# A pool of its own for the whole gates' tiles in a gated hybrid attention block

## The chip, the cores and the metric

The kernel runs on one core of one Trainium2 chip. The metric is the device time of one execution in microseconds (us). The engines are TensorE (PE in the profile, PEld its weight loads), VectorE (DVE), ScalarE (ACT), GpSimd (POOL) and SyncE (SP, which here issues the DMAs). SBUF is the on-chip memory of 128 partitions; PSUM holds the matmuls' results in 8 banks of 128 x 512 fp32.

## The reference

One transformer block in fp32 on 1024 tokens of width 1024. Three attention branches of width 512 run on the normed input: A, a differential attention of 4 heads; B, a dilated window attention with three groups of 4 heads, whose outputs are mixed by the softmax of their log-sum-exps; and C, an attention to 256 memory slots. Each branch has a projection to the full width and a sigmoid gate for every channel; the gated sum goes through an output matrix, and a SwiGLU feed-forward part follows.

```python
wts = jax.nn.softmax(jnp.stack(lses, axis=2), axis=2)                       # the merge of B
out_b = jnp.sum(wts[..., None].astype(bv.dtype) * jnp.stack(outs, axis=2), axis=2)
...
branches = jnp.einsum('btgc,gcd->btgd', jnp.stack([out_a, out_b, out_c], axis=2), w_branch[l])
gates = jax.nn.sigmoid(h @ w_gate[l] + b_gate[l]).reshape(b, t, N_BRANCHES, d)
x = x + jnp.sum(gates * branches, axis=2) @ w_out[l]
h2 = rms_norm(x, norm_ffn[l])
x = x + (jax.nn.silu(h2 @ w_ffn_gate[l]) * (h2 @ w_ffn_up[l])) @ w_ffn_down[l]
```

## The kernel before, in words

Activations are kept transposed: 8 tiles of 128 channels by 1024 tokens, in two halves c of 512. An fp32 operand is split into a rounded high part and a low remainder (`split`, L257: ACT casts the high part at L259, another engine subtracts at L260; for weights L156 and L157), and a product takes three matmuls for each pair of operands (L191 to L193). A pair of high and low is a tile of 4 KB a partition, called `t4`, and the pools `big` (16 tiles) and `a4` (20 tiles) hold such tiles.

The work goes through the input projections, the gates' products (their sums before the sigmoid are stored in DRAM, `gates[n]`, 24 arrays of 512 KB), the attentions C, A and B, the branch projections, the output matrix and the feed-forward part. Products of branches A and C run among the heads of B as fillers.

At the end of each of B's four heads comes the merge (L975 to L1003). Its small weights go to DRAM and come back spread over all partitions as one tile `W` of 128 x 3072 (L998, 1.5 MB). DVE multiplies three head tiles `u` by it (L1000), adds them in two steps (L1002), and the sum is spilled to DRAM (L1003). After the fourth head the pools of the attention are closed (`att.close()`, L1006), and the pools `pb` (6 PSUM banks), `ev` and `a4` are allocated in the memory that they leave.

Then `gated_first(d)` (L1094) runs for d = 0 to 7. It loads two whole gates into tiles of `a4` (`whole_gate`, L1088: the DMA at L1090, the sigmoid on ACT at L1091), multiplies the mix, which holds branch A, by the first (L1097), evicts two banks of branch C's product from PSUM times the second (L1099), and adds that to the mix (L1100). With 2 banks of another pool there are 8, so the products of four values of d fit before an eviction must free one; a block d takes 24 matmuls. After it comes branch B for c = 0: its input `oT[1, k, c]` is loaded from the spill (L1147, tile `c`) and split on ACT and POOL; its gates are loaded for each half (L1072), and evicted at L1085 and added at L1086. The output weights `wo[d]` (L1112) and the feed-forward's operands `h2` follow in `big` and `a4`. In the last stage (`down`, seven products over 11 pairs of k of the matrix w_fd) the right operands take tiles of `a4` as well, beside 8 tiles of w_fd itself, loaded at L1227.

The order of instructions on each engine is set when the program is built: a scheduler simulates the work and orders each engine's instructions by it, taking a wait for memory into account where a new tile covers the bytes of an old one. On the chip each engine goes through its list in order. All DMAs of this part are issued by SP in one queue, and their completions are told by 8 semaphores in turn.

In the built program of before, W of the last merge takes bytes 146,624 to 158,912 of each partition and `a4` begins at 146,944. The tiles of the first and the seventh d's first loads lie at 146,944 and 151,040, inside W's bytes.

Of the kernel before, what the change touches and what calls it, by code (L numbers as in the profile page):

```python
# [30 lines left out]
LAMBDA_INIT = 0.8 - 0.6  # L31
BIG = 1e30

A4 = 20
EV_BUFS = {"g": 5, "s": 4, "c": 2, "ws": 2}

EARLY = 3
# [40 lines left out]
def hybrid_block_kernel(ctx: ExitStack, tc: tile.TileContext, xT, memT, w_ab, w_cq, w_kv,  # L78
# [3 lines left out]
    def pool(name, bufs=1, space=None, stack=ctx):  # L82
        kw = {} if space is None else {"space": space}
        if space is not DRAM:
            kw["reuse_waits"] = "tile"
        return stack.enter_context(tc.tile_pool(name=name, bufs=bufs, **kw))
# [14 lines left out]
    V, G = nc.vector, nc.gpsimd  # L101
# [25 lines left out]
    gx, gf = (const.tile([P, KT], F32, name=f"g{m}") for m in "xf")  # L127
# [37 lines left out]
    big = pool("big", 16)  # L165
# [91 lines left out]
    def split(dst, src, eng):  # L257

        nc.scalar.copy(dst[:, 0], src)  # L259
        eng.tensor_sub(dst[:, 1], src, dst[:, 0].bitcast(F32))  # L260
# [57 lines left out]
    with ExitStack() as pst:  # L318
# [196 lines left out]
        for u in (U_AV, *range(U_AQK, U_AQK + 4, 2), *range(U_BV, U_BV + 6, 2), *range(U_BQK, U_BQK + 12, 2)):  # L515
# [9 lines left out]
            if u in (U_BV, U_BV + 2, U_BV + 4):  # L525
                x = ("T1", "T3", "T4")[(u - U_BV) // 2]
# [54 lines left out]
    def early_sum():  # L581
        return wp.tile([P, 512], F32, name="eg", bufs=3)
# [204 lines left out]
    with ExitStack() as st:  # L787
# [8 lines left out]
        mix, oT = [], {}  # L796
# [57 lines left out]
        for h in range(BH):  # L854
            st_mc = bp.tile([P, 3, 2, 8], F32, name="mc", bufs=2)
            U = []
            for g in range(3):
# [58 lines left out]
                elif g == 1:  # L916
                    for q4 in range(2):
                        op = ps_tile(opp, "op")
                        for r2 in range(2):
                            r = 2 * q4 + r2  # L920
# [87 lines left out]

    pb = pool("pb", 6, PSUM)
    ev = pool("ev")  # L1010
    a4 = pool("a4", A4)
    turn = [0]

# [4 lines left out]
    def t4(pl, dt=F32R):  # L1018
        return pl.tile([P, 2, 512], dt, name="t4")

    def t2(name):
        return ev.tile([P, 512], F32, name=name, bufs=EV_BUFS[name])
# [5 lines left out]
    def right(pl, src, eng):  # L1028
        t = t4(pl)
        split(t, src, eng)  # L1030
        return t

    def rights(blocks, pls, gain, scale):

        rs, t2s = {}, []
        n = len(blocks)

        def make(name, srcs):  # L1040
            rs[name] = [right(pls[name][i], x, V) for i, x in enumerate(srcs)]

        for i, ((b11, b12), (b21, b22)) in enumerate(blocks):
            for b, g in ((b12, i), (b22, i + n)):
                V.scalar_tensor_tensor(out=b, in0=b, scalar=gain[:, g:g + 1], in1=scale, op0=ALU.mult, op1=ALU.mult)
            V.tensor_sub(b11, b12, b11)
            t2s.append(t2("s"))
            V.tensor_sub(t2s[-1], b22, b11)
            rs.setdefault("T2", []).append(right(pls["T2"][i], t2s[-1], V))
        for (b11, b12), (b21, b22) in blocks:  # L1050
            V.tensor_sub(b12, b22, b12)
        make("T3", [b[0][1] for b in blocks])
        for i, ((b11, b12), (b21, b22)) in enumerate(blocks):
            V.tensor_sub(b21, t2s[i], b21)
        make("T4", [b[1][0] for b in blocks])
        make("T1", [b[0][0] for b in blocks])
        make("22", [b[1][1] for b in blocks])
        return rs
# [7 lines left out]
    def blocks_of(ts_):  # L1066
        return [[[t[:, c] for c in range(2)] for t in p_] for p_ in ts_]
# [8 lines left out]
    x1 = mix  # L1076
# [26 lines left out]
    mh, wo, pss = {}, {}, {}  # L1103
# [4 lines left out]
    def load_out(d):  # L1108

        raw = wp.tile([P, 1024], F32, name="raw", bufs=3)  # L1110
        nc.sync.dma_start(out=raw.rearrange("p (k m) -> p k m", m=P), in_=w_out[d])
        wo[d] = [right(a4, raw[:, i * 512:(i + 1) * 512], G) for i in range(2)]  # L1112

    def out_block(d, c):

# [16 lines left out]
    def row_scale(c):  # L1132
        return rsqrt(ev, pss[c][0], D, [P, 512], ("g", "g"), EV_BUFS["g"])

    h2 = {"11": [], "21": []}

    def norm_first(k, r, rst):
        i = k + 4 * (r == "21")
        V.scalar_tensor_tensor(out=x1[i][:, 0], in0=x1[i][:, 0], scalar=gf[:, i:i + 1], in1=rst, op0=ALU.mult, op1=ALU.mult)
        h2[r].append(right(big if k % 2 else a4, x1[i][:, 0], V))  # L1140

    for d in range(KT):
        gated_first(d, load_pieces(w_br[2 * KT + d], 4, P))
    for c in range(2):
        for k in range(4):
            o = t2("c")
            nc.sync.dma_start(out=o, in_=spill[1][:, k, CS[c]])  # L1147
            oT[1, k, c] = right(a4, o, G)
    for d in range(KT):
        gated(1, d, 0, load_pieces(w_br[KT + d], 4, P))  # L1150
        split_mix(d, 0, big)
    for d in range(KT):
        load_out(d)
        out_block(d, 0)
        gated(1, d, 1, load_pieces(w_br[KT + d], 4, P))
# [3 lines left out]
    rst = row_scale(0)  # L1159
    for n, d in enumerate(reversed(range(KT))):  # L1160
        out_block(d, 1)
        norm_first(n % 4, ("11", "21")[n // 4], rst)
# [50 lines left out]
    rst = row_scale(1)  # L1213
# [1 line left out]
        low[0] = V if f else G  # L1215
        ahead(f)
    bl = blocks_of([(x1[k], x1[k + 4]) for k in range(4)])
    h2 |= rights(bl, {**{x: [a4] * 4 for x in ("T2", "T1", "T3", "T4")}, "22": [big] * 4}, gf, rst)


    wd, groups = {}, [range(k, min(k + 2, HF)) for k in range(0, HF, 2)]
# [73 lines left out]
    for d, ps in enumerate(down("T1", s1_of)):  # L1295
        V.tensor_add(u3s[d], ps, u3s[d])
        store_out(1, d, 1, u3s[d], G)
        x = early_sum()
# [91 lines left out]
```

## Time and profile before

| what | value |
|---|---|
| three runs | 2110.09, 2111.51, 2114.27 us |
| median | 2111.51 us |
| the profiled execution | 2107.51 us, of it 2105.7 us span |
| granted TensorE clock, mean | 0.985 |
| busy, share of the span | PE 95%, PEld 82%, DVE 65%, ACT 44%, POOL 53% |
| DMA traffic | 300.37 MB, mean 143 GB/s |

How to read it: times of single instructions come from the profiled execution, which is one run of its own; the median is over three other runs. Busy shares are means over the whole span, in which the stages differ. The clock is told as a share of 2.4 GHz, and 0.5 is 1.2 GHz. A row of the chain of waits names what the end of the program was waiting for at that moment, in order of time.

### The profile page before, as it was taken

How to read it: one execution, taken by the hardware profiler on the slowest of the kernel's cores; microseconds unless marked ns; L12 is line 12 of the kernel's file. 1: busy time of each engine (PE TensorE's matmuls, PEld its weight loads, DVE VectorE, ACT ScalarE, POOL GpSimd, SP SyncE). 2: the span in 40 equal slices, each digit the busy share in tenths (PEclk: the TensorE clock that was granted, in tenths of full speed). 3: DMA queues.
4: the chain of work that ended last, by engine and by line, in shares of the span. 5: the costliest groups of instructions: out<-in, count | busy, mean ns of one | idle time of the engine just before them, and what ended most of it. 6: DMA issues, size and time to landing. Idle time of an engine off the chain costs nothing.

```text
span 2105.7 us, 31371 instructions
## 1 busy us (share of the span) xinstructions
PE 1990.1 (95%) x11384; PEld 1716.8 (82%) x11384; DVE 1363.7 (65%) x2148; ACT 917.0 (44%) x1839; POOL 1114.4 (53%) x766
## 2 busy tenths in 40 slices
PE   6799999999999889899989997999999999999999
PEld 5799999999977677678768785777788888888887
DVE  8975543566575799997354436633977667579961
ACT  5434322344344566664535655532523323344441
POOL 5685644666753576665445223820165554545764
PEclk9899999999999999999999998999999999999999
DMA  6263343323143333254866537642344323255441
GB/s 228 82 214 111 106 141 115 101 91 131 71 161 128 122 113 97 80 162 152 265 228 221 174 112 281 198 144 80 136 146 149 106 85 125 96 174 216 145 152 69
DMA packets 134730, 300.37 MB, mean 143 GB/s; under 512 B 19120, under 2 KB 43184, under 8 KB 134064
## 3 DMA queue, kind: packets, MB, share of 16 engines
q1 hardware_dynamic: 134576, 298.37, 42.0%
q8 instruction: 90, 1.47, 0.3%
q14 instruction: 64, 0.52, 0.1%
HBM read 204.58 MB, written 89.54 MB: 140 GB/s over the span
## 4 chain that ended last, share of the span: by engine, by line
PE 40%; DVE 4%; DMA 3%; issue 1%; ACT 1%; POOL 1%; SPq 0%; DVEq 0%; ACTq 0%; POOLq 0%
PE pb L191 9%; PE pb L193 9%; PE pb L192 9%; PE mm L191 4%; PE mm L192 4%; PE mm L193 4%; DMA W<-wd 1%; DVE u L1000 1%; PE mm L1130 1%; PE op L939 1%; DVE t L1086 0%; PE tp L293 0%; DVE t L260 0%; DVE u L1002 0%; PE op L910 0%
## 5 line engine op out<-in xcount | busy, mean ns | idle before, releaser
L211 POOL TENSOR_TENSOR wl<-raw,wh 128x512 fp32r<-128x512 f32 x204 | 282.0, 1394 | 186.4 <-ACT wh L210 163.4
L191 PE MATMUL pb<-t,wh 128*128 128x512 f32 x795 | 308.4, 391 | 15.2 <-DVE t L1099 15.2
L192 PE MATMUL pb<-t,wh 128*128 128x512 f32 x795 | 310.9, 392 | 1.9 <-DVE t L260 1.9
L193 PE MATMUL pb<-t,wl 128*128 128x512 f32 x795 | 311.0, 391 | 0.0
L191 PE MATMUL mm<-t,wh 128*128 128x512 f32 x657 | 265.0, 404 | 7.9 <-ACT wh L210 5.4
L193 PE MATMUL mm<-t,wl 128*128 128x512 f32 x657 | 260.1, 397 | 1.2 <-POOL wl L211 1.2
L192 PE MATMUL mm<-t,wh 128*128 128x512 f32 x657 | 260.8, 397 | 0.0
L210 ACT CAST wh<-raw 128x512 fp32r<-128x512 f32 x216 | 129.9, 618 | 205.3 <-PE pb L192 95.8
L191 PEld LDWEIGHTS pb<-t,wh 128*128 128x128 f32 x795 | 150.1, 189 | 47.3 <-DVE t L1099 15.7
L480 PE MATMUL sp<-wh,t 128*128 128x256 f32 x672 | 188.2, 280 | 0.0
L479 PE MATMUL sp<-wl,t 128*128 128x256 f32 x672 | 188.2, 280 | 0.0
L478 PE MATMUL sp<-wh,t 128*128 128x256 f32 x672 | 188.2, 280 | 0.0
L192 PEld LDWEIGHTS pb<-t,wh 128*128 128x128 f32 x795 | 150.3, 189 | 34.0 <-DVE t L260 2.3
L193 PEld LDWEIGHTS pb<-t,wl 128*128 128x128 f32 x795 | 150.0, 189 | 31.7 <-issue 0.5
L191 PEld LDWEIGHTS mm<-t,wh 128*128 128x128 f32 x657 | 124.8, 190 | 35.8 <-ACT wh L210 7.5
L193 PEld LDWEIGHTS mm<-t,wl 128*128 128x128 f32 x657 | 124.8, 190 | 28.4 <-POOL wl L211 1.6
L192 PEld LDWEIGHTS mm<-t,wh 128*128 128x128 f32 x657 | 124.8, 190 | 25.8 <-issue 0.5
L465 POOL TENSOR_TENSOR wl<-ws,wh 128x512 fp32r<-128x512 f32 x72 | 101.4, 1430 | 60.8 <-ACT wh L464 47.5
L211 POOL TENSOR_TENSOR wl<-ws,wh 128x512 fp32r<-128x512 f32 x21 | 30.2, 1439 | 184.8 <-ACT wh L210 184.8
L480 PEld LDWEIGHTS sp<-wh,t 128*128 128x128 f32 x672 | 127.8, 190 | 0.0
L478 PEld LDWEIGHTS sp<-wh,t 128*128 128x128 f32 x672 | 127.8, 190 | 0.0
L479 PEld LDWEIGHTS sp<-wl,t 128*128 128x128 f32 x672 | 127.8, 190 | 0.0
(436 smaller groups left out, 5320.7 us busy)
## 6 DMA issues: line engine op xcount, KB each, us to landing
proj<-nat SPq DMA_DIRECT2D x48, 512.0 KB, 2.7
raw<-in_w_gate SPq DMA_DIRECT2D x36, 512.0 KB, 3.6
nat<-proj SPq DMA_DIRECT2D x32, 512.0 KB, 4.4
raw<-in_w_fg SPq DMA_DIRECT2D x25, 512.0 KB, 4.1
raw<-in_w_fu SPq DMA_DIRECT2D x25, 512.0 KB, 3.6
raw<-in_w_ab SPq DMA_DIRECT2D x24, 512.0 KB, 3.9
rawp<-in_w_ab SPq DMA_DIRECT2D x24, 512.0 KB, 5.7
t<-in_w_fd SPq DMA_DIRECT2D x20, 512.0 KB, 7.3
```

The source lines that it names most:

```text
L191: nc.tensor.matmul(ps, lhsT=wh, rhs=rh, start=start, stop=False)
L192: nc.tensor.matmul(ps, lhsT=wh, rhs=rl, start=False, stop=False)
L193: nc.tensor.matmul(ps, lhsT=wl, rhs=rh, start=False, stop=stop)
L210: nc.scalar.copy(wh, src)
L211: low[0].tensor_sub(wl, src, wh.bitcast(F32))
L465: nc.gpsimd.tensor_sub(wl, r, wh.bitcast(F32))
L478: nc.tensor.matmul(ps[:, i], lhsT=aH, rhs=wh, start=k == 0, stop=False)
L479: nc.tensor.matmul(ps[:, i], lhsT=aH, rhs=wl, start=False, stop=False)
L480: nc.tensor.matmul(ps[:, i], lhsT=aL, rhs=wh, start=False, stop=k == 3)
L939: nc.tensor.matmul(op[:, r2 * 256:(r2 + 1) * 256], lhsT=vt[:, 2 * r + k], rhs=pT[:, 2 * k:2 * k + 2], start=k == 0, stop=k == 1)
L1000: nc.vector.tensor_mul(U[g], U[g], W[:, g])
L1130: nc.tensor.matmul(pss[c][0], lhsT=ones, rhs=sq, start=pss[c][1] == 1, stop=pss[c][1] == KT)
```

## The change

`a4` gets 16 tiles, and a new pool `a4x` of 4 tiles is allocated ahead of it. Other tiles go to `a4x`: the output weights of d = 6 and 7, branch B's inputs of c = 0, the even feed-forward operands of the quadrant "11", and two operands of "T1". The whole gates stay in `a4`. Nothing is computed in another way. In the built program `a4x` takes bytes 146,944 to 163,328, and `a4` 163,328 to 228,864, so the first gate's tile now lies at 163,328, behind W. Lines behind L1010 stand two numbers higher.

```diff
-A4 = 20
+A4 = 16
...
     ev = pool("ev")
+
+    a4x = pool("a4x", 4)
     a4 = pool("a4", A4)
...
-        wo[d] = [right(a4, raw[:, i * 512:(i + 1) * 512], G) for i in range(2)]
+        wo[d] = [right(a4 if d < 6 else a4x, raw[:, i * 512:(i + 1) * 512], G) for i in range(2)]
...
-        h2[r].append(right(big if k % 2 else a4, x1[i][:, 0], V))
+        h2[r].append(right(big if k % 2 else a4x if r == "11" else a4, x1[i][:, 0], V))
...
-            oT[1, k, c] = right(a4, o, G)
+            oT[1, k, c] = right(a4 if c else a4x, o, G)
...
-    h2 |= rights(bl, {**{x: [a4] * 4 for x in ("T2", "T1", "T3", "T4")}, "22": [big] * 4}, gf, rst)
+    h2 |= rights(bl, {**{x: [a4] * 4 for x in ("T2", "T3", "T4")}, "T1": [a4x] * 2 + [a4] * 2, "22": [big] * 4}, gf, rst)
```

The queue of SP at the last merge, before. W is its weights, `t_` a whole gate's tile, `raw` a weight tile of branch B, `u_` the merged head.

```order
L998 DMA W<-wd 128x3072
L146 DMA raw<-in_w_br 128x512 x2
L1003 DMA spill_59<-u_13240 128x1024
L146 DMA raw<-in_w_br 128x512
L1090 DMA t_14005<-gate_7115 128x1024
L1090 DMA t_14008<-gate_7131 128x1024
```

The same queue after the change, at its two ends: the first gates, and the end of the 16.

```order
L998 DMA W<-wd 128x3072
L1092 DMA t_14008<-gate_7115 128x1024
L1092 DMA t_14011<-gate_7131 128x1024
...
L1092 DMA t_14305<-gate_7138 128x1024
L146 DMA raw<-in_w_br 128x512 x3
L1003 DMA spill_59<-u_13240 128x1024
L146 DMA raw<-in_w_br 128x512
L1149 DMA c<-spill_59 128x512 x2
```

The 16 gate loads have moved ahead of the merged head's store and of three weight loads.

DVE at the last merge, before; `t_13438` is the mix of d = 0, `pb` a PSUM bank.

```order
L1000 TENSOR_TENSOR u_13653<-u_13653,W 128x1024
L1002 TENSOR_TENSOR u_13240<-u_13240,u_13494 128x1024
L1002 TENSOR_TENSOR u_13240<-u_13240,u_13653 128x1024
L1097 TENSOR_TENSOR t_13438<-t_13438,t_14005 128x1024
L1099 TENSOR_TENSOR t_14008<-pb,t_14008 128x512 x2
```

DVE there after the change.

```order
L1000 TENSOR_TENSOR u_13653<-u_13653,W 128x1024
L1002 TENSOR_TENSOR u_13240<-u_13240,u_13494 128x1024
L1099 TENSOR_TENSOR t_13438<-t_13438,t_14008 128x1024
L1002 TENSOR_TENSOR u_13240<-u_13240,u_13653 128x1024
L1101 TENSOR_TENSOR t_14011<-pb,t_14011 128x512 x2
```

The mix times gate 0 has moved ahead of the merge's second addition.

ACT in the same place, before; `oa` is branch C's input, `wh` a weight's high part.

```order
L259 CAST t_13978<-oa 128x512
L156 CAST wh<-raw 128x512 x4
L1091 ACT_TABLE_LOAD
L1091 ACTIVATE t_14005<-t_14005,pk 128x1024
L1091 ACTIVATE t_14008<-t_14008,pk 128x1024
```

ACT there after the change.

```order
L259 CAST t_13978<-oa 128x512
L1093 ACT_TABLE_LOAD
L1093 ACTIVATE t_14008<-t_14008,pk 128x1024
L156 CAST wh<-raw 128x512 x2
L1093 ACTIVATE t_14011<-t_14011,pk 128x1024
L156 CAST wh<-raw 128x512
```

The table load and the first sigmoid have moved ahead of the weight casts, and the second sigmoid between them.

## Rows read from the trace of the kernel before

**Rows 1.** Waits of TensorE: engine line waited for: total, times, longest

```profile
PE pb L191 <- DVE t L1099: 15.2, 1, 15.2
```

**Rows 2.** Windows: stretch us, busy (count) by engine, clock, DMA share, GB/s

```profile
1280.00:1290.00 10.00, 0.00 (x0) 0.00 (x0) 3.03 (x2) 0.96 (x1) 0.72 (x1) 0.55 0.59 215
1290.00:1300.00 10.00, 6.61 (x20) 5.25 (x20) 8.45 (x10) 8.87 (x9) 0.00 (x0) 0.60 1.03 419
```

**Rows 3.** Chain of waits, 1264 to 1294: start us, us, what ran

```profile
1266.27 7.30 DMA W<-wd
1273.59 6.01 DVE u L1000 x3
1279.60 2.21 DVE u L1002
1281.84 1.24 DVE u L1002
1283.09 0.33 SPq L1003
...
1283.98 5.00 DMA t<-gate
1289.04 1.24 ACT L1091
1290.34 1.16 ACT t L1091
...
1292.66 0.69 DVE t L1099
1293.39 0.79 PE pb L191
```

**Rows 4.** Timeline of SP, 1262 to 1308: start us, us, instructions

```profile
1274.09 2.57 SPq L146 DMA_DIRECT2D raw<-in_w_br  x2
...
1283.98 14.12 SPq L1090 DMA_DIRECT2D t<-gate  x16
1298.99 1.56 SPq L1147 DMA_DIRECT2D c<-spill  x2
```

**Rows 5.** Lines L1090 and L998: transfers from issue to landing

```profile
DMA to landing us min/median/max: 7.0/9.5/10.0
...
DMA to landing us min/median/max: 7.3/8.3/9.3
```

**Rows 6.** Timelines of DVE and POOL; line L1002: ns min/median/max

```profile
1223.69 3.50 DVE L1000 TENSOR_TENSOR u<-u,W 128x1024 f32<-128x1024 f32 x3 [3.40 <-DMA W<-wd]
...
L1002 DVE TENSOR_TENSOR u<-u,u x8: 1216/1488/2277, 1092.6 to 1281.8; 128x1024 f32<-128x1024 f32 x8
...
1272.77 5.76 POOL L157 TENSOR_TENSOR wl<-raw,wh 128x512 fp32r<-128x512 f32 x3 [2.91 <-PE mm L193]
...
1228.72 1.34 POOL L157 TENSOR_TENSOR wl<-raw,wh 128x512 fp32r<-128x512 f32 x1 [13.65 <-ACT wh L156]
```

**Rows 7.** Timeline of ACT, 1262 to 1345

```profile
1272.07 1.14 ACT L156 CAST wh<-raw 128x512 fp32r<-128x512 f32 x2 [3.57 <-PE pb L192]
...
1290.34 8.61 ACT L1091 ACTIVATE t<-t,pk 128x1024 f32<-128x1024 f32 x8
...
1312.29 1.12 ACT L259 CAST t<-c 128x512 fp32r<-128x512 f32 x2
```

**Rows 8.** Timeline of DVE after the wait

```profile
1291.52 1.23 DVE L1097 TENSOR_TENSOR t<-t,t 128x1024 f32<-128x1024 f32 x1 [8.45 <-ACT t L1091]
```

**Rows 9.** Windows of 2 us at the wait

```profile
1282.00:1284.00 2.00, 0.00 (x0) 0.00 (x0) 1.06 (x1) 0.00 (x0) 0.00 (x0) 0.50 0.06 25
...
1298.00:1300.00 2.00, 2.00 (x11) 1.62 (x9) 2.00 (x3) 0.95 (x1) 0.00 (x0) 0.99 1.02 418
```

**Rows 10.** A window of the down stage; line L1227's transfers to landing

```profile
1920.00:1940.00 20.00, 20.00 (x90) 16.55 (x89) 20.00 (x21) 9.30 (x17) 10.77 (x7) 1.00 0.53 206
...
DMA to landing us min/median/max: 4.2/7.7/9.6
```

## The prediction

> **What bounds the kernel now.** I read the page first: TensorE (PE) is busy for nearly the whole span, so only what makes PE stand still, or what lengthens its own work, can move the end. Then the list of what PE waited for. Its longest wait is a single one of 15.2 us, of a product's first matmul (L191, into a bank of pool pb) on the VectorE (DVE) instruction of L1099 [rows 1]. The change touches just the tiles of that line, so the question is how much of these 15.2 us goes. The windows of 10 us show where it lies: from 1280 to 1290 PE has 0.00 us of work while the 16 DMA engines are busy 59% of the time, and in the next ten it works 6.61 of them, at a mean clock of 0.60 [rows 2].
>
> The chain of waits tells what fills the gap [rows 3]. The weights W of the fourth head's merge land at 1273.57 (1266.27 + 7.30). DVE multiplies three tiles by them (6.01 us), adds twice (2.21 and 1.24), and is through at 1283.09. Only then does the first whole gate's load start: it is the wait for memory, since the first gate tile lay on bytes that W occupied. Its load takes 5.00 us on the chain, ScalarE's (ACT) table load 1.24 and the sigmoid 1.16; DVE multiplies the mix by it, and then the first eviction (0.69) frees a bank, and PE restarts at 1293.39. The 16 gate loads stand together on the queue of SP, from 1283.98, and the two loads of the spilled head behind them [rows 4]. So the 10.3 us from 1283.09 to 1293.39 are load, sigmoid and first evictions, one after another, and nothing but addresses puts them behind the merge.
>
> **The change part by part.** *The gates' loads.* The gate tiles no longer share a byte with W. In SP's order the 16 loads now stand right behind the load of W. Each gate is 512 KB, and in the window from 1290 the queue moves 419 GB/s [rows 2], so one lands every 1.25 us; the 7.0 to 10.0 us from issue to landing are mostly the time in line behind others [rows 5]. W, ahead of them in the same queue, is taken to land at 1273.57 as before, gate 0 at about 1274.8, the second at 1276.1, the sixteenth at 1293.6.
>
> *The sigmoids.* ACT: 1274.8 + 1.24 (table) + 1.16 = 1277.2. In ACT's new order this stands ahead of two weight casts which ran at 1272.07 [rows 7]. They take 1.14 us and end at 1278.3, and the second gate's sigmoid ends at about 1279.5.
>
> *DVE.* Its order becomes: three multiplications by W, one addition, the mix by gate 0, the second addition, the eviction. From 1273.59 there are two prices. In the third head, where GpSimd (POOL) had been idle for 13.65 us until 1228.72, the three multiplications took 3.50 us; in the fourth they took 6.01, and in that stretch POOL ran three splits for 5.76 us [rows 6]. The additions take between 1.2 and 2.3 us [rows 6], the mix by the gate 1.23 with POOL idle [rows 8]. All fast: 3.50 + 1.24 + 1.23 + 1.24 + 0.69 = 7.90, and PE restarts at 1281.5. All as slow as seen here: 6.01 + 2.21 + 1.23 + 1.24 + 0.69 = 11.38, and PE restarts at 1285.0. Since POOL's splits follow the casts, they move from 1272.77 to about 1277.8. I therefore take the multiplications at 3.50 (to 1277.1), and the two additions and the mix, which now have POOL beside them, at 2.0, 2.2 and 1.7, between their two prices: 1283.0, and with the eviction 1283.7.
>
> The rows show a slowdown when POOL and DVE run together, but not which DVE instructions suffer. The Trainium skill, page "GPSIMD Engine Reference", section "Specifications", says that GpSimd's SBUF interface is shared with VectorE, and contends with DVE instructions that have two SBUF inputs. By that rule the additions and the mix would all be hit (about 2.3 us each) and the eviction, which reads PSUM, would not: 3.50 + 6.9 + 0.69 = 11.1, PE at 1284.7, 1.0 us later than I say.
>
> So the gain is 1293.39 − 1283.7 = 9.7 us, between 8.4 and 11.9.
>
> *The clock.* In the gap the granted clock is at half, 0.50 (1.2 GHz), and it is back at 0.99 in the window from 1298 [rows 9]; PE had worked about 4.6 us at half rate by then, which costs 2.3 us. The new gap is still some 5.5 us (from 1293.4 − 15.2 = 1278.2 to 1283.7), so I charge the same 2.3 us again: no gain. If the clock holds, up to 2.3 more are gained.
>
> *What now stands behind the gates.* Three weight loads of branch B (two of them were issued at 1274.09 [rows 4]), the store of the merged head and the loads of it (c) come behind 16 gates on SP. They land at about 1295.5 (weights), 1298 (the store) and 1302 (c). ACT's cast of c stood behind the last sigmoid, at 1312.29 [rows 7]; the sixteen sigmoids, 8 of which took 8.61 us, now end at about 1297. With a cast and a split on POOL, c is ready at about 1305. PE needs it when branch C's last four blocks are done: 96 matmuls at 90 to 20 us [rows 10] are 21.3, with 2.3 for the clock 1283.7 + 23.6 = 1307.3. So it is covered, by 2.3 us only; 0, with 2 us of loss as the other end. Below nothing it can't be: none of these loads comes earlier.
>
> *The smaller pools.* a4 has 16 tiles for 20, and four tiles that were shared now serve only output weights, branch B's input and right operands. In the down stage fewer a4 tiles are free for right operands beside the 8 of w_fd. PE is at 20.00 of 20 us there while it runs [rows 10], so a tile that comes free a few us later is hidden: 0, with 2 us either way, as the reordered stretches may shed or add small waits.
>
> *The sum.* Own time of the profiled execution 2107.5 (its span is 2105.7, 1.8 lie around it); 2107.5 − 9.7 = 2097.8. The median of the runs is 2111.5, 4.0 above the profiled one. The forecast is made for the median: 2111.5 − 9.7 = 2101.8 us.
>
> **The rivals.**
> *The gates delay W (no change).* The eight loads in flight share the 16 DMA engines with W. If they shared evenly, W would land when they do, 8 × 1.25 = 10 us later, at about 1283.6; the DVE chain of 7.9 to 11.4 us follows and PE restarts between 1291.5 and 1295, so about 2111. For it: W took 7.3 to 9.3 us in its four loads [rows 5]. Against it: the gates themselves, all in flight together, land one after another in order of issue, as the sigmoids run one per 1.08 us (8.61 / 8) [rows 7]. In a sentence by itself: the Trainium skill, "DMA: Bandwidth & Descriptors", section "Queues, rings and completion order", says that descriptors of one queue start in order on each engine while completions need not be; by that W's data go first and this rival falls, and the sum stays where it is.
>
> *The small pool starves the down stage (slower).* The six loads of the last quarter of w_fd need tiles of a4, and the right operands draw on the same pool: 8 free ones where there were 12. One right operand lasts 12 matmuls, 2.7 us, so the look-ahead shrinks from 32 to 22 us. If the six loads then come only as tiles come free, the first is late by its landing of 7.7 us [rows 10], and each of the next five by 7.7 less the 5.4 us that PE has from a pair: 7.7 + 5 × 2.3 = 19.2 us, 2101.8 + 19.2 = 2121. It decides from the point at which fewer than three tiles are free (3 × 2.7 = 8.1 us, about one landing). Against it: eight are, and 22 us of look-ahead is near three landings.
>
> *The change doesn't do what it says.* Some other byte of the merge, or another wait of the first gate, holds it as before: 2111.5. Against it: in the new order the mix by gate 0 stands ahead of the merge's last addition, which only a gate loaded earlier makes useful.
>
> **How the numbers follow.** Forecast 0.87, W delayed 0.06, starved down stage 0.04, no effect 0.03. A difference under 0.2% (4.2 us) can't be told from no change here. The forecast's own ends: 8.4 to 11.9 of gain, up to 2.3 of the clock, 2 each for branch B and the later stages, so 2095.6 to 2107.1; a partial delay of W, by the 2.0 us between its fastest and slowest landing, lies in that too. I leave out the lowest 1 us, where all favours would have to meet, and stretch the top toward the rivals: 2096.5 to 2107.5. Faster by over 0.2%: 0.84 (0.03 of the forecast may end inside the bound); within: 0.12; slower: 0.04.
>
> **What would show it.** In the profile after: the first gate's load issued within a microsecond of W's, not after the store of the merged head; W landing at the same distance from its issue; the table load about 1.3 us behind W's landing; the multiplications by W near 1.2 us each and the additions near 2; PE's longest wait on the first eviction down from 15.2 to about 5.5 us; the clock at half for some microseconds all the same; no new wait of PE on the split of c; no new wait in the down stage. It would be wrong if W's landing moved, if the first evictions waited for ACT rather than DVE, or if a wait of some 10 us showed up at branch B.

## The result, and the profile after

| kernel | median us | runs | ratio to before (95% interval) |
|---|---|---|---|
| before | 2110.02 | 6 (2105.24 to 2114.27) | 1 |
| changed | 2099.85 | 6 (2097.56 to 2100.83) | 0.995 (0.9936 to 0.9965) |

The change makes the kernel 10.2 us faster in these runs; it was forecast at 9.7, and at 2101.8 us. Timed twice more beside other kernels it had 0.9963 (0.9949 to 0.9977) and 0.9967 (0.9954 to 0.9980), 8.0 and 5.9 us below before. The profiled execution has a span of 2095.8 us (2105.7 before). PE's longest wait of [rows 1] is now (engine, line waited for: total, times, longest):

```profile
PE pb L191 <- DVE t L1101: 6.0, 1, 6.0
```

The windows that answer to [rows 2] (busy us of PE, PEld, DVE, ACT, POOL, then clock, DMA share, GB/s) show PE at work from 1282, DVE without a pause, and the DMA engines full:

```profile
1270.00:1280.00 10.00, 6.22 (x28) 4.82 (x26) 7.50 (x6) 6.22 (x8) 3.20 (x2) 1.00 1.00 404
1280.00:1290.00 10.00, 7.79 (x23) 6.22 (x24) 10.00 (x12) 9.61 (x9) 2.69 (x2) 0.66 1.03 420
```

On SP's queue (start, duration) the first of the 16 gate loads follows W at once, and the store of the merged head and the loads of c come behind them; compare [rows 4]:

```profile
1264.46 0.32 SPq L998 DMA_DIRECT2D W<-wd  x1
1264.87 19.36 SPq L1092 DMA_DIRECT2D t<-gate  x16
...
1288.94 0.33 SPq L1003 DMA_DIRECT2D spill<-u  x1
...
1299.31 0.90 SPq L1149 DMA_DIRECT2D c<-spill  x2
```

The row of 16 hides a pause. Between the first gate and the second SP waited, for 2.0 us of it on POOL's split of branch C's input, so that seven of the first eight gates were issued only from 3.5 us after W on (the last row: who waited, for what, total, times, longest):

```profile
1264.87 0.38 SPq L1092 DMA_DIRECT2D t<-gate  x1
1267.94 0.32 SPq L1092 DMA_DIRECT2D t<-gate  x1
...
SPq L1092 <- POOL t L260: 2.0, 1, 2.0
```

DVE's timeline answers to the middle of [rows 3] and to [rows 6, 8]. W has landed at 1272.50, 8.04 us after its issue. The three multiplications take 3.50 us, the first addition 1.22, then the mix by gate 0 takes 2.30 and the second addition 2.29; the first evictions begin at 1281.47. The last row is the last eviction of branch C, the first instruction since 1272.50 before which DVE was idle:

```profile
1272.50 3.50 DVE L1000 TENSOR_TENSOR u<-u,W 128x1024 f32<-128x1024 f32 x3 [9.74 <-DMA W<-wd]
1275.91 1.22 DVE L1002 TENSOR_TENSOR u<-u,u 128x1024 f32<-128x1024 f32 x1
1277.05 2.30 DVE L1099 TENSOR_TENSOR t<-t,t 128x1024 f32<-128x1024 f32 x1
1279.27 2.29 DVE L1002 TENSOR_TENSOR u<-u,u 128x1024 f32<-128x1024 f32 x1
1281.47 1.27 DVE L1101 TENSOR_TENSOR t<-pb,t 128x512 f32<-128x512 f32 x2
...
1306.89 0.69 DVE L1101 TENSOR_TENSOR t<-mm,t 128x512 f32<-128x512 f32 x1 [0.60 <-PE mm L193]
```

ACT has its table load and first sigmoid ahead of the casts, as its order said, and its first cast of c comes at 1302.41 (1312.29 in [rows 7]):

```profile
1273.76 1.28 ACT L1093 ACT_TABLE_LOAD   x1 [7.22 <-DMA t<-gate]
1275.06 1.15 ACT L1093 ACTIVATE t<-t,pk 128x1024 f32<-128x1024 f32 x1
1276.12 1.12 ACT L156 CAST wh<-raw 128x512 fp32r<-128x512 f32 x2
1277.14 1.15 ACT L1093 ACTIVATE t<-t,pk 128x1024 f32<-128x1024 f32 x1
...
1302.41 0.62 ACT L259 CAST t<-c 128x512 fp32r<-128x512 f32 x1
```

POOL's first three splits, at 1272.77 in [rows 6], run from 1276.80 to 1282.69, beside the two slow DVE instructions. The next four take 11.17 us, and the splits of c come after them:

```profile
1276.80 5.89 POOL L157 TENSOR_TENSOR wl<-raw,wh 128x512 fp32r<-128x512 f32 x3 [8.88 <-ACT wh L156]
1295.68 11.17 POOL L157 TENSOR_TENSOR wl<-raw,wh 128x512 fp32r<-128x512 f32 x4 [12.99 <-ACT wh L156]
1306.81 3.53 POOL L260 TENSOR_TENSOR t<-c,t 128x512 fp32r<-128x512 f32 x2
```

The clock, against [rows 9]: half level again after the shorter wait, and full from 1288. A second dip follows a wait of 1.98 us at 1334.69:

```profile
1282.00:1284.00 2.00, 1.79 (x4) 1.49 (x5) 2.00 (x4) 2.00 (x3) 0.69 (x1) 0.50 1.03 422
...
1288.00:1290.00 2.00, 2.00 (x11) 1.62 (x10) 2.00 (x3) 1.94 (x2) 0.00 (x0) 1.00 1.01 416
...
1336.00:1338.00 2.00, 2.00 (x7) 1.52 (x6) 2.00 (x3) 1.01 (x2) 2.00 (x2) 0.50 0.73 222
```

Executions differ ahead of the changed stretch, where the programs are the same: W of the last head was issued between 1264.46 and 1272.01 us in the profiles of the changed kernel. Two profiles are therefore best compared from that issue on. From it to PE's restart: 27.12 us before (1293.39 − 1266.27), 17.75 after (1282.21 − 1264.46), so 9.4 gained. From it to the end of the span: 839.4 before (2105.7 − 1266.27), 831.3 after, so 8.1 gained; in the two later profiles of the changed kernel 8.0 and 7.6.

### The profile page after: what moved, and what is told of

It is laid out like the page before. It is cut to its first block, busy times and chain, and to the rows that moved or that the text cites. A ratio compares the mean times of both kernels' runs of the same rounds, so it can differ in the third digit from the quotient of the medians.

```text
span 2095.8 us, 31384 instructions
## 1 busy us (share of the span) xinstructions
PE 1991.3 (95%) x11384; PEld 1718.6 (82%) x11384; DVE 1355.0 (65%) x2148; ACT 918.0 (44%) x1839; POOL 1116.3 (53%) x766
## 3 DMA queue, kind: packets, MB, share of 16 engines
q1 hardware_dynamic: 134576, 298.37, 42.4%
## 5 line engine op out<-in xcount | busy, mean ns | idle before, releaser
L211 POOL TENSOR_TENSOR wl<-raw,wh 128x512 fp32r<-128x512 f32 x204 | 283.4, 1401 | 183.2 <-ACT wh L210 158.8
L157 POOL TENSOR_TENSOR wl<-raw,wh 128x512 fp32r<-128x512 f32 x49 | 80.8, 1664 | 88.8 <-ACT wh L156 68.8
```

The costliest lines, as they stand in the source:

```text
L157: lo.tensor_sub(wl, r, wh.bitcast(F32))
L211: low[0].tensor_sub(wl, src, wh.bitcast(F32))
```

## The experiments

**Is it the addresses?** The extra pool is allocated behind the other:

```diff
-    a4x = pool("a4x", 4)
     a4 = pool("a4", A4)
+    a4x = pool("a4x", 4)
```

Expected:

> The changed kernel, with the extra pool of four tiles allocated behind the pool of 16 instead of ahead of it: the same split into two pools, but the whole gates' tiles again begin on the bytes of the last merge's weights W. If the gain is one of addresses alone, it is all gone: the gate loads follow the merge, PE's longest wait is about 15 us, the time about 2110 us. If the split itself helps (fewer tiles that wait for each other), about 2100 us and a wait of 6 us.

Measured 2108.94 us, ratio 1.0002 (0.9991 to 1.0014). SP's queue is that of before again (W at 1264.90, the gates 0.9 us behind the store of the merged head), and PE's wait on the first eviction is back:

```profile
1264.90 0.32 SPq L998 DMA_DIRECT2D W<-wd  x1
...
1281.76 0.33 SPq L1003 DMA_DIRECT2D spill<-u  x1
...
1282.65 14.11 SPq L1092 DMA_DIRECT2D t<-gate  x16
```

```profile
PE pb L191 <- DVE t L1101: 15.3, 1, 15.3
```

So the split into two pools gives nothing and costs nothing that can be measured; the whole gain is that the gates' tiles lie off W's bytes. From W's issue to the end of the span it has 839.6 us, as before.

**What keeps the gates from delaying W?** The last head's W is loaded from ACT's queue:

```diff
-            nc.sync.dma_start(out=W, in_=wd[None, :, :].broadcast_to([P, 3, T]))
+            (nc.scalar if h == 3 else nc.sync).dma_start(out=W, in_=wd[None, :, :].broadcast_to([P, 3, T]))
```

Expected:

> The changed kernel, with the last head's W loaded from ACT's queue instead of SP's. It tests why the gates did not delay W. If it is their place behind W in the same queue, W now shares the DMA engines with eight gates: at half of 420 GB/s its 1.5 MB take 7.5 us and a fixed part of about 2, so 9.5 to 10 us to landing instead of 8.0, up to 16 if it gets one share in nine; gate 0 lands earlier, and the time is 2101 to 2108 us. If W is bound by its own reading and the place in the queue plays no part, 8.0 us as now, and 2100.

Measured 2101.24 us, 0.9963 (0.9950 to 0.9976), as for the changed kernel. W was issued at 1269.30, 0.7 us behind the first gate on SP, and DVE had it at 1277.09, after 7.79 us. ACT had gate 0 at 1273.29, 4.7 us after its issue, and the second gate at 1278.70:

```profile
1269.30 0.35 ACTq L998 DMA_DIRECT2D W<-wd  x1
...
1273.29 1.28 ACT L1093 ACT_TABLE_LOAD   x1 [1.24 <-DMA t<-gate]
...
1278.70 1.16 ACT L1093 ACTIVATE t<-t,pk 128x1024 f32<-128x1024 f32 x1 [1.93 <-DMA t<-gate]
```

The time of W is that of the second expectation, and the median, at the edge of the first one's range, decides nothing, as the changed kernel's own medians lie between 2099.85 and 2104.64. But the run tests less than it was meant to. SP issued the second gate only at 1273.46, after 2.4 us of waiting on a load of branch C's input and 2.0 us on POOL's split of it:

```profile
1268.62 0.38 SPq L1092 DMA_DIRECT2D t<-gate  x1
1273.46 0.32 SPq L1092 DMA_DIRECT2D t<-gate  x1
```

So the second gate was late because it was issued late: ACT had it 5.2 us after its issue. Of the gates W shared the DMA engines with one at first, and with more only in its last 3.6 us. That one gate ahead of it, on another queue, cost it at most half a microsecond (7.79 us for 7.30 before). What eight gates in flight from the start would cost W, in the same queue or in another, no run here shows, since in the changed kernel too SP paused behind the first gate. Whether W's place in the queue protects it stays open.

**What makes the mix and the second addition slow?** For three of branch B's weights POOL's split is left out and the high part stands in for the low:

```diff
+                if lo is not None:
-                lo.tensor_sub(wl, r, wh.bitcast(F32))
+                    lo.tensor_sub(wl, r, wh.bitcast(F32))
-                pieces.append((wh, wl))
+                pieces.append((wh, wh if lo is None else wl))
...
-        gated(1, d, 0, load_pieces(w_br[KT + d], 4, P))
+        gated(1, d, 0, load_pieces(w_br[KT + d], 4, P, ((nc.scalar.copy, None if d < 3 else nc.gpsimd),)))
```

Expected:

> The changed kernel without POOL's three splits that fall on the merge: for the first three weight pieces of branch B the low part is not computed and the high part stands in its place. If POOL's work is what slows DVE's mix (2.30 us) and second addition (2.29), both take 1.22, PE waits about 3.9 us instead of 6.0, and the time is about 2097.7 us. If the gates' DMA traffic slows them, they stay at 2.3, and the time at 2100.

Measured 2098.67 us, 0.9949 (0.9930 to 0.9967). The mix (L1100 here) and the second addition (L1003) take 1.22 us each while the gates still load, and PE waits 3.58 us. The last row is the window at that place (busy us of PE, PEld, DVE, ACT, POOL, then clock, DMA share, GB/s):

```profile
1279.55 1.22 DVE L1100 TENSOR_TENSOR t<-t,t 128x1024 f32<-128x1024 f32 x1
1280.68 1.22 DVE L1003 TENSOR_TENSOR u<-u,u 128x1024 f32<-128x1024 f32 x1
...
1280.00:1282.00 2.00, 0.00 (x0) 0.00 (x0) 2.00 (x3) 2.00 (x3) 0.00 (x0) 0.92 1.04 424
```

POOL is the cause, not the DMA traffic, which is as heavy as it was (424 GB/s, 420 in the changed kernel). The run with W on ACT's queue says the same with nothing left out: there POOL's splits fell on the multiplications by W, which took 6.05 us, and the mix and the second addition, with POOL idle and 424 GB/s of DMA, took 1.21 each:

```profile
1277.09 6.05 DVE L1000 TENSOR_TENSOR u<-u,W 128x1024 f32<-128x1024 f32 x3 [9.49 <-DMA W<-wd]
...
1284.20 1.21 DVE L1099 TENSOR_TENSOR t<-t,t 128x1024 f32<-128x1024 f32 x1
1285.33 1.21 DVE L1002 TENSOR_TENSOR u<-u,u 128x1024 f32<-128x1024 f32 x1
```

The sum of the rows was nearly right too: 2.15 us less of DVE's work, and W 0.25 us sooner after its issue (7.79 for 8.04), make PE's wait 2.4 us shorter. From W's issue to the end of the span it has 828.1 us, 3.2 to 3.7 less than the changed kernel's profiles. The medians don't show this gain by themselves, since the interval of the ratio spans the changed kernel's three ratios, 0.995, 0.9963 and 0.9967.

**Is it DVE's order that is left?** In gated_first the gate of branch C is loaded first, and its banks are evicted before the mix is multiplied:

```diff
-        g0, g2 = whole_gate(d), whole_gate(2 * KT + d)
-        V.tensor_mul(mix[d], mix[d], g0)
+        g2, g0 = whole_gate(2 * KT + d), whole_gate(d)
         for c in range(2):
             V.tensor_mul(g2[:, c], branch(2, d, c, wb), g2[:, c])
+        V.tensor_mul(mix[d], mix[d], g0)
```

Expected:

> The changed kernel, with gated_first written in another order: the second gate is loaded first, and branch C's banks are evicted before the mix is multiplied by its gate. If what is left of the wait is DVE's order (addition, mix, addition, then the eviction), the first eviction ends 3.50 + 1.22 + 0.69 = 5.4 us after W lands instead of 9.7, PE waits about 1.7 us instead of 6.0, and the time is about 2095.5 us; if the clock then also stays at full level, about 2093. If the wait is bounded by something else by then (the sigmoid, another wait of the banks), no gain: 2100.

Measured 2104.16 us, 0.9974 (0.9963 to 0.9986): no gain over the changed kernel, whose ratios are lower, and 832.4 us from W's issue to the end of the span for its 831.3 to 831.8. The first eviction is early, as expected, and PE waits 1.44 us there. But two new waits follow:

```profile
1278.97 0.50 PE L191 MATMUL pb<-t,wh 128*128 128x512 f32 x1 [1.44 <-DVE t L1100]
...
1305.23 0.51 PE L191 MATMUL pb<-t,wh 128*128 128x512 f32 x1 [2.86 <-DVE t L1100]
1309.65 0.80 PE L191 MATMUL pb<-t,wh 128*128 128x512 f32 x1 [3.92 <-DVE t L1100]
```

They are on evictions that now stand behind a multiplication of the mix on DVE, each 2.28 us because POOL splits c and a weight at the same time:

```profile
1302.29 2.28 DVE L1101 TENSOR_TENSOR t<-t,t 128x1024 f32<-128x1024 f32 x1
1304.50 0.68 DVE L1100 TENSOR_TENSOR t<-pb,t 128x512 f32<-128x512 f32 x1
...
1306.71 2.28 DVE L1101 TENSOR_TENSOR t<-t,t 128x1024 f32<-128x1024 f32 x1
1308.92 0.68 DVE L1100 TENSOR_TENSOR t<-pb,t 128x512 f32<-128x512 f32 x1
```

The same order for d = 0 alone:

```diff
-        g0, g2 = whole_gate(d), whole_gate(2 * KT + d)
-        V.tensor_mul(mix[d], mix[d], g0)
+        g2 = whole_gate(2 * KT + d) if d == 0 else None
+        g0 = whole_gate(d)
+        if d:
+            g2 = whole_gate(2 * KT + d)
+            V.tensor_mul(mix[d], mix[d], g0)
...
+        if d == 0:
+            V.tensor_mul(mix[d], mix[d], g0)
```

Expected:

> The changed kernel, with the new order (gate of branch C first, evict before the mix is multiplied) for d = 0 alone; the other seven as in the changed kernel. If PE's first wait is what counts, PE restarts 5.4 us after W lands instead of 9.7, the wait is 1.4 us, and 4 to 6 us are gained: 2094 to 2096. If DVE, which in the changed kernel works without a pause from W's landing to the last evictions of branch C, sets the end of this stretch, the wait only comes back behind it, and the gain is below 1 us: 2099 to 2100.

Measured 2105.99 us, 0.9981 (0.9972 to 0.9990), beside 0.9963 (0.9949 to 0.9977) for the changed kernel on the same chip: the first of the two expectations falls, and even the second, of a gain below 1 us, was too good. The two intervals still touch, but the profile agrees: 834.2 us from W's issue to the end of the span, 2.4 to 2.8 more than the changed kernel's. PE's one wait of 6 us has become five, with 7.8 us in all:

```profile
PE pb L191 <- DVE t L1104: 7.8, 5, 2.4
```

The changed kernel itself, timed beside it:

> The changed kernel unaltered, timed beside the next two on one chip: about 2099.9 us, ratio to before 0.995, PE's wait on the first eviction 6.0 us.

Measured 2101.72 us. Its profile has a wait of 5.62 us on the first eviction, and one that the first profile lacks, on POOL's split of c at the start of branch B:

```profile
1316.15 0.50 PE L192 MATMUL pb<-t,wh 128*128 128x512 f32 x1 [1.51 <-POOL t L260]
```

**POOL's splits over the whole stretch.** All eight low parts of branch B's first half are left out (`None if d < 3 else nc.gpsimd` becomes `None`).

Expected:

> The changed kernel without any of POOL's eight weight splits of branch B's first half (the high part stands in for the low part). If POOL's splits slow DVE over the whole stretch of branch C, its multiplications and additions are all near 1.21 us until the splits of c begin, and the time is 3 to 4 us below the changed kernel's: about 2096. If only the first 2 us of it matter, as without three of them, 2098 to 2099.

Measured 2099.92 us, 0.9958 (0.9944 to 0.9972). DVE's instructions are all near 1.22 us until POOL splits c, and the last eviction of branch C comes 38.7 us after W's issue (1306.94 − 1268.25), against 42.4 in the changed kernel (1306.89 − 1264.46); 0.6 of these 3.7 us is W's own load, 7.42 us here. But the 3 to 4 us are not seen in the time, 1.8 us below the changed kernel's median with overlapping intervals, nor from W's issue to the end of the span, where it has 829.2 us, 2.2 to 2.6 less; new waits behind it (1.00 us on ACT's cast of c at 1307.91, 1.28 at 1340.96) take part of it. The expectation was right for the stretch, and not borne out for the end.

**Less for DVE to do behind W.** Instead of another order, W is loaded in three pieces:

```diff
-            nc.sync.dma_start(out=W, in_=wd[None, :, :].broadcast_to([P, 3, T]))
+            for g in range(3):
+                nc.sync.dma_start(out=W[:, g], in_=wd[None, g].broadcast_to([P, T]))
```

The changed kernel again, as the one to compare with:

> The changed kernel unaltered, timed beside the next two on one chip: about 2101 us; from W's landing to the end of the span 823.4 us, as in its two profiles so far.

Expected of the three pieces:

> The changed kernel, with the weights W of each of the four merges loaded in three pieces of 512 KB instead of one of 1.5 MB, so that DVE's first two multiplications and the first addition can run while the rest is still under way. If DVE bounds the stretch from W to branch C's last evictions, its work behind the last piece is 3 x 1.2 us shorter, PE's first wait falls from 6.0 to about 3 us and the gain stays: 3 us, about 2098 us. If the stretch is bound elsewhere, the wait only moves, as it did with the early eviction: 2100 to 2102.

In three pieces for the last head only:

> As the one before, with W in three pieces for the last head only. The same 3 us if they come from the last merge (about 2098 us); a difference between the two is what the first three heads give or cost.

| kernel, one chip | median us | ratio to before (95% interval) |
|---|---|---|
| changed | 2104.64 | 0.9967 (0.9954 to 0.9980) |
| W in three, all heads | 2097.80 | 0.9936 (0.9924 to 0.9948) |
| W in three, last head | 2099.31 | 0.9943 (0.9931 to 0.9955) |

The unaltered kernel had 823.9 us from W's landing to the end, near the expected 823.4. With three pieces for all heads the median is the lowest of all, and its interval lies below that of the changed kernel timed beside it; it overlaps the changed kernel's first one (0.9936 to 0.9965), measured at another time. In the version for the last head DVE has the first piece 4.90 us after its issue at 1270.49, and the first addition runs between the second and the third multiplication; PE's first wait is 2.97 us:

```profile
1275.39 1.23 DVE L1003 TENSOR_TENSOR u<-u,W 128x1024 f32<-128x1024 f32 x1 [6.59 <-DMA W<-wd]
1277.41 1.23 DVE L1003 TENSOR_TENSOR u<-u,W 128x1024 f32<-128x1024 f32 x1 [0.79 <-DMA W<-wd]
1278.67 1.22 DVE L1005 TENSOR_TENSOR u<-u,u 128x1024 f32<-128x1024 f32 x1
1279.81 1.22 DVE L1003 TENSOR_TENSOR u<-u,W 128x1024 f32<-128x1024 f32 x1
...
1284.52 1.29 DVE L1104 TENSOR_TENSOR t<-pb,t 128x512 f32<-128x512 f32 x2 [0.85 <-DMA t<-gate]
```

```profile
1285.27 0.50 PE L191 MATMUL pb<-t,wh 128*128 128x512 f32 x1 [2.97 <-DVE t L1104]
```

The eviction now waits for the second gate (0.85 us of idle time ahead of it), not for DVE. The row names the gate's load, but what ended last is its sigmoid on ACT, at 1284.49, which ran without a pause behind the table load, the first sigmoid and two weight casts:

```profile
1283.35 1.14 ACT L1096 ACTIVATE t<-t,pk 128x1024 f32<-128x1024 f32 x1
```

From W's issue to the end of the span it has 829.2 us, 2.1 to 2.6 less than the changed kernel's three profiles; for all heads it is 830.6, with a new wait of 2.15 us on POOL's split of c at 1308.65. The medians say 5.3 and 6.8 us. What gives the rest, and whether the first three heads gain anything, these runs don't tell.

## Why the prediction was right, point by point

*Addresses put the gates behind the merge.* Shown by the swapped pools: with the gates back on W's bytes all of the gain goes, with the pools' sizes as changed. The third rival (no effect) and the second (a starved down stage) fall with it; PE has no wait above 1.3 us behind 1400 in the profile after.

*W lands as before.* Nearly. Its load took 7.30 us before and 7.27 with the pools swapped, and 8.04, 7.91 and 7.89 in the three profiles of the changed kernel, 0.6 to 0.7 us more; the sum had this at nothing. In four other runs with the gates behind W it took 7.42 to 8.07, so how much of it is due to the gates is not shown. The first rival's delay of 10 us did not come, but its condition did not come either: SP paused behind the first gate, and the other seven were issued 3.5 to 6.1 us after W in these profiles. I had all eight in flight from the start. My reason, the place in the queue, was not tested by this, and neither was it by W on the other queue. Nor do the back-to-back sigmoids that I read against this rival show it: at 1.08 us each, about the time that one takes (1.15), they run so whether the gates land one by one or together.

*The DVE chain.* From W's landing to PE's restart I had 10.1 us, and it was 9.71. The multiplications came to 3.50 as taken. For the two additions I had 2.0 and 2.2 and for the mix 1.7, in all 5.9; the additions took 1.22 and 2.29 and the mix 2.30, in all 5.8. POOL began only 0.3 us before the end of the first addition, which my own times could have told (POOL from 1277.8, a fast addition until 1278.3). The first addition was 0.8 too long in the sum and the mix 0.6 too short, and that the two nearly cancel is luck. That POOL and not the DMA traffic is the cause was argued then and is shown now. The rule of the Trainium skill ("GPSIMD Engine Reference", "Specifications") agrees with these rows where POOL was at work: the instructions with two SBUF inputs took 2.3 us, and two evictions from PSUM together 1.27, as they do alone. Its sum of 11.1 was too long by 1.4, of which the first addition is 1.1 (2.3 for 1.22), and the rest that neighbouring rows overlap a little.

*The clock.* Charged again, as said. PE stood for 5.99 us, and ran at half level from 1282.21 to about 1287.6, 5.4 us where it had been 4.6: 0.4 us more lost, none gained.

*Branch B's input.* c was to be ready at 1305, and POOL was through with it at 1310.34, because the four weight splits ahead of it took 2.8 us each beside a busy DVE. The cover of 2.3 us was gone, then. PE did not wait for it in the first profile, and 1.51 us in the second; the bound of 2 us held.

*What was given back.* At PE's restart, which is what the sum was about, 9.4 us were gained for a forecast of 9.7. That the first median's gain, 10.2 us, is so near 9.7 is partly luck: the two repeats gave 8.0 and 5.9, and the three profiles, from W's issue on, 8.1, 8.0 and 7.6. The lowest time of the forecast's own ends was added up wrongly as well (2111.5 − 11.9 − 2.3 − 2 is 2095.3, not 2095.6), which changes nothing. 9.4 us at PE's restart became 8.1 at the end. PE's waits behind the restart of over 0.3 us sum to 7.9 us after, and to 7.1 before; with 0.4 for the clock that is 1.1 of the 1.3 us. The half-level stretch before 1510 in before is gone, and one at 1336 has come.

*What I had not seen.* In the changed kernel DVE bounds the stretch from W to branch C's last eviction. It works without a pause for 34 us there, and both early evictions show that PE, restarted sooner, only meets it again. The prediction treated branch C as PE's own work of 23.6 us. The error did not show in the first profile because there, after a wait of 6 us, PE and DVE come out of the stretch together, DVE with 0.60 us to spare. It shows in the third profile of the unaltered kernel, where PE waits a second time on one of these evictions:

```profile
1316.13 0.50 PE L191 MATMUL pb<-t,wh 128*128 128x512 f32 x1 [1.74 <-DVE t L1101]
```

## What to carry to other kernels

When a pool is opened on memory that another stage still reads, look at which of the new tiles lie on the late bytes: the first loads of the next stage should get the bytes that came free first. Then add up the work of each engine from the last input of the old stage to the end of the new one; where one engine is busy throughout, as DVE was here, moving its instructions only moved the wait, and what helped was to let it start earlier, by loading its input in pieces. Compare two profiles from the last common event, since what lies ahead can differ by more than the effect.

## What the runs showed of the hardware that was not expected

- A VectorE instruction on two SBUF tiles of 128 x 1024 goes from 1.21 to 1.7 or 2.3 us while GpSimd splits, and GpSimd's split of 128 x 512 from 1.3 to 1.9 or 2.8 us; evictions from PSUM keep 0.64 to 0.68 us.
- A broadcast load of 1.5 MB took 7.79 us when it was issued from a second queue, 0.7 us behind one 512 KB load of the first; in the first queue, with 512 KB loads issued behind it, it took 7.42 to 8.07 us in seven profiles. The 512 KB load was usable after 4.7 us there, and after 8.9 us (1273.76 − 1264.87) behind the 1.5 MB in one queue.
- The same program reached the same load at 1264.5, 1271.5 and 1272.0 us of its span in three profiled executions.
